# Second block's input projection by Strassen's scheme in 16 of its 18 pairs of column blocks, and its two output projections streamed from DRAM over eight PSUM banks

## The chip, the cores and the metric

One core of a Trainium2 chip runs the whole program. The metric is the device time of one execution in microseconds. The program computes two transformer-like blocks on 1024 positions of width 1024, in float32, with each float32 product made of three matrix products of split operands. Only the middle of the second block is touched here.

## The reference, cut to what matters

```python
def second_block(x, ...):
    h = rms_norm(x, g_mix_pre)
    z = h @ w_in                              # 1024 x 1024 by 1024 x 4608
    u_pool, u_rx, u_rg = z[..., :512], z[..., 512:1536], z[..., 1536:2560]
    gate_pool = sigmoid(z[..., 2560:3584]); gate_rnn = sigmoid(z[..., 3584:])
    y_pool = pool_mixer(u_pool, ...) @ w_pool_out        # 512 wide, by 512 x 1024
    y_rnn = rg_lru_branch(u_rx, u_rg, ...) @ w_rg_out    # 1024 wide, by 1024 x 1024
    x = x + rms_norm((gate_pool * y_pool + gate_rnn * y_rnn) @ w_o, g_mix_post)
    ...                                       # FFN and a last gated term follow

def rg_lru_branch(xb, gb, ...):
    xc = causal_dwconv(xb, conv_w, conv_b)               # 4 taps along the positions
    r, i = sigmoid(xc @ w_gates[0] + b0), sigmoid(xc @ w_gates[1] + b1)   # per head of 64
    log_a = -8 * r * softplus(-lru_lambda); a = exp(log_a)
    u = sqrt(1 - exp(2 * log_a)) * i * xc
    h[t] = a[t] * h[t-1] + u[t]                          # along the positions
    return h * gelu(gb)
```

## The kernel before

Every float32 operand of TensorE is split into a high part, written by ScalarE (`split`, L86), and a low part, made by VectorE as the difference (L89). One product of a 128x128 piece of weights with 512 positions is three matmuls (`mm3`, L341 to L343). Weights come from DRAM into raw buffers (`wr`) through SP's queue, are split into `wh` and `wl`, and a buffer is loaded again as soon as its reader lets it go (`need`, `free`, `pump`). Activations lie transposed, positions along the free axis, as `h2h` and `h2l`. The code is written in Python; a scheduler puts the instructions into one static order for each engine, and each engine then runs its own in that order, waiting on semaphores.

The second block's mixer works on column blocks of `w_in`, 128 columns each, with 8 pieces of 128 rows. A block costs 2 halves of 512 positions x 8 pieces x 3 = 48 matmuls. There are 36 blocks.

- `mixer` (L2041): 16 blocks in pairs, the input `rx` and the gate `gb` of one of 8 groups of recurrent channels, then 4 blocks of the pooling input. `rx` is evicted by ScalarE at L2059, `gb` through a gelu at L2065. After each pair `rnn_chain` (L1917) runs for its 128 channels: a short convolution `xc` (ScalarE L1927, three VectorE operations L1930), its split into `xch` and `xcl`, 12 small matmuls for the two gates, sigmoids (L1943), exp, tanh and square root on ScalarE, a scan on VectorE (L1959), and the product with `gb` on GpSimd (L1960), stored to `zz_d` in DRAM. `pool_chain` (L1964) does the pooling blocks and has 2 float32 matmuls of its own (L1986) for each.
- `mix_gates` (L2071): 16 blocks of gates, through a sigmoid (L2076) to `sg2_d` in DRAM. Meanwhile the 12 pieces of `zz_d` come back and are split into `zh` and `zl`, which hold all of z in SBUF.
- `mix_out` (L2081): for each of 8 output blocks and each half of the positions, 4 pieces of `w_pool_out` and 8 of `w_rg_out`, 576 matmuls in all. Each of the two sums is multiplied with its gate on VectorE (L2109), the two are added (L2111) and split into `m2h`, `m2l`.
- `mix_add` (L2142) multiplies by `w_o`, adds and norms; then `ffn_up` (L2171) starts.

The second half of `ffn_up` already computes pairs of column blocks by a scheme of Strassen's kind. Two column blocks by two halves of the rows of the weights, and two halves of the positions, make a 2x2 problem that takes 7 products of 12 matmuls instead of 8: 84 for 96. In exchange GpSimd makes sums of weights (`wsum`, L238, called S with two operations and D with three), which are split on ScalarE (L227) and VectorE (L228), and the products are combined by two evictions on ScalarE (L2235, L2239), four additions that read PSUM on VectorE and two additions on GpSimd (L2230). The four parts of the weights of a pair are called u, s, d and v. The sums of the activations (`ft1` to `ft3`, and the fourth in place) are made once by `fast_operands` (L262, operations L271 and L272).

Of the kernel before, what the change touches and what calls it, by code (L numbers as in the profile page):

```python
# [16 lines left out]
F32 = mybir.dt.float32  # L18
# [10 lines left out]
P = 128  # L29
# [38 lines left out]
class Kernel:  # L68
# [193 lines left out]
    def fast_operands(self, pool, tmp):  # L262
# [41 lines left out]
        self.fast_last = last  # L304

# [1611 lines left out]
    def rnn_chain(self, pool, c, rx, gb):  # L1917

        nc = self.nc
        t = lambda name, bufs=1, n=S: pool.tile([P, n], F32, name=name, tag=name, bufs=bufs)  # L1920
        wbd = pool.tile([P, 2, P], F32, name="wbd", tag="wbd", bufs=2)
# [4 lines left out]
        xc = t("xc", 2)  # L1926
        nc.scalar.activation(xc, rx[:, 3:], AF.Identity, scale=self.conv_w[:, 24 + c:25 + c],  # L1927
# [4 lines left out]
        xh, xl = (pool.tile([P, S], F32R, name=n, tag=n, bufs=1) for n in ("xch", "xcl"))  # L1932
        self.split(xh, xl, xc)
        wh, wl = (pool.tile([P, 2, P], F32R, name=n, tag=n, bufs=2) for n in ("wgh", "wgl"))
        self.split(wh, wl, wbd)
        yield 6.0
        g = [t("rg0", n=S + 16), t("rg1", n=S + 16)]
# [26 lines left out]
    def pool_chain(self, pool, g, u):  # L1964
# [4 lines left out]
        pw = pool.tile([P, P], F32, name="pw", tag="pw", bufs=2)  # L1969
# [12 lines left out]
        y = pool.tile([P, S], F32, name="py", tag="gb", bufs=2)  # L1982
# [58 lines left out]
    def mixer(self, pl, chunks):  # L2041

        nc = self.nc
        self.sg2_d = self.dram.tile([16, P, S], F32, name="sg2_d")
        self.zz_d = self.dram.tile([12, P, S], F32, name="zz_d")
# [3 lines left out]
        us = {}  # L2049

        def emit(b, half, ps):
            hs = slice(half * 512, half * 512 + 512)
            c = b // 2
            if b < 16 and b % 2 == 0 or b >= 16:
                pad = 3 if b < 16 else 16
                if half == 0:
                    us[b] = pl.tile([P, pad + S], F32, name="rx", tag="rx", bufs=2)
                    nc.gpsimd.memset(us[b][:, :pad], 0.0)
                nc.scalar.activation(us[b][:, pad + half * 512:pad + half * 512 + 512], ps, AF.Copy)  # L2059
                if half and b >= 16:  # L2060
                    self.later_steps(1.0, self.pool_chain(pl, b - 16, us.pop(b)))
            else:
                if half == 0:
                    us[b] = pl.tile([P, S], F32, name="gb", tag="gb", bufs=2)
                nc.scalar.activation(us[b][:, hs], ps, AF.Gelu_apprx_tanh)  # L2065
                if half:
                    self.later_steps(1.0, self.rnn_chain(pl, c, us.pop(b - 1), us.pop(b)))

        return self.dense_t_steps(chunks, self.hT, emit, first=4)

    def mix_gates(self, pl, chunks):  # L2071
        nc = self.nc

        def emit(b, half, ps):
            sg = pl.tile([P, 512], F32, name="sg2", tag="sg2", bufs=2)
            nc.scalar.activation(sg, ps, AF.Sigmoid)  # L2076
            self.later(1.0, lambda: nc.sync.dma_start(self.sg2_d[b, :, half * 512:half * 512 + 512], sg))

        return self.dense_t_steps(chunks, self.hT, emit)

    def mix_out(self, pool, z, chunks, mT):  # L2081

        nc = self.nc
        sgs = []

        def load(n):
            b, half, i = n // 4, n // 2 % 2, n % 2
            sg = pool.tile([P, 512], F32, name="mg", tag="mg", bufs=6)
            nc.sync.dma_start(sg, self.sg2_d[8 * i + b, :, half * 512:half * 512 + 512])
            sgs.append(sg)  # L2090

        for n in range(4):
            load(n)
        for b in range(KT):
            for half in range(2):
                hs = slice(half * 512, half * 512 + 512)
                m = []
                for i, k0 in enumerate((0, 4)):
                    c = chunks[2 * b + i]
                    n = c.shape[1]  # L2100
                    wh, wl = self.need(c)
                    ps = self.mmt()
                    for k in range(n):
                        self.mm3(ps, (wh[:, k], wl[:, k]), (z[0][:, k0 + k, hs], z[1][:, k0 + k, hs]),
                                 k == 0, k == n - 1)
                    if half:
                        self.free(c)
                    sg = sgs.pop(0)
                    nc.vector.tensor_tensor(sg, ps, sg, op=OP.mult)  # L2109
                    m.append(sg)  # L2110
                nc.vector.tensor_add(m[0], m[0], m[1])  # L2111
                self.split(mT[0][:, b, hs], mT[1][:, b, hs], m[0])
                n = 4 * b + 2 * half + 4
                if n < 32:
                    load(n)
                    load(n + 1)
# [54 lines left out]
    def ffn_up(self, pu, up, pairs, es_t, near_end):  # L2171
# [46 lines left out]
        x = self.fast  # L2218

        def product(chunk, o, m):  # L2220
            ps = self.mmt()
            wh, wl = self.need(chunk)
            for k in range(4):
                self.mm3(ps, (wh[:, o + k], wl[:, o + k]), (m[0][:, k], m[1][:, k]), k == 0, k == 3)
            return ps

        for c, (u, s, d, v) in enumerate(pairs, len(up) // 2):
            if c == NC - 2:
                near_end()
            add = lambda e, out, p, q: e.tensor_tensor(out, p, q, op=OP.add)  # L2230
            s1, s2, s3, s5 = (pu.tile([P, 512], F32, name=n, tag=n) for n in ("fs1", "fs2", "fs3", "fs5"))
            new(c)
            g = st[c]
            up0, up1 = (us[c % 2][:, 2 + n * 512:514 + n * 512] for n in range(2))
            nc.scalar.activation(s1, product(u, 0, x["b11"]), AF.Copy)  # L2235
            add(nc.vector, up0, s1, product(u, 4, x["b21"]))
            self.free(u)
            gate(c, 0, up0)
            nc.scalar.activation(s5, product(s, 0, x["t1"]), AF.Copy)  # L2239
            add(nc.vector, s2, s1, product(s, 4, x["t2"]))  # L2240
            self.free(s)
            add(nc.vector, s3, s2, product(d, 0, x["t3"]))
            add(nc.gpsimd, s2, s2, s5)
            add(nc.gpsimd, s5, s3, s5)
            add(nc.vector, up1, s2, product(d, 4, x["b22"]))
            self.free(d)
            gate(c, 1, up1)
            add(nc.vector, s3, s3, product(v, 0, x["t4"]))
            self.free(v)
            nc.vector.tensor_tensor(g[:, half(0)], s3, g[:, half(0)], op=OP.mult)  # L2250
            nc.gpsimd.tensor_tensor(g[:, half(1)], s5, g[:, half(1)], op=OP.mult)
            store(c)
# [18 lines left out]
    def block2(self, es):  # L2271
# [3 lines left out]
        ch_a, es_w, es_c = self.mix_ch, self.es_w, self.es_c  # L2275
        ch_g = [self.chunk_t(blk(wi, 2560 + P * b), KT) for b in range(16)]

        es_h, es_p = (ExitStack() for _ in range(2))
# [3 lines left out]
        with es_c:  # L2282
# [5 lines left out]
            self.queue(ch_a[1:2])  # L2288
# [4 lines left out]
        pl = self.pool(es_p, "mixp")  # L2293
        self.queue(ch_a[2:] + ch_g)
        steps = self.mixer(pl, ch_a)
        for _ in steps:
            pass
        gates = self.mix_gates(sp, ch_g)
        while self.chains or not self.drained("mixw"):
            next(gates)  # L2300
        ch_m = []
        for b in range(KT):
            for w, n in ((a["w_pool_out_2"][0], 4), (a["w_rg_out_2"][0], 8)):
                ch_m += self.chunks_t([blk(w, b * P)], n)
        w = a["w_o_2"][0]
        ch_o = [self.chunks_n(w[:, c * 512:c * 512 + 512], KT, 512) for _ in range(2) for c in range(2)]
        es_p.close()
        es_w.close()

        es_z, es_m = ExitStack(), ExitStack()  # L2310
        zp = self.pool(es_z, "zp")
        z = [zp.tile([P, 12, S], F32R, name=n) for n in ("zh", "zl")]
        k = 0
        with ExitStack() as es2:
            zr = self.pool(es2, "zraw")
# [260 lines left out]
```

## Time and profile before

| what | value |
|---|---|
| median of 3 runs | 3472.66 us (3471.07 to 3474.35) |
| the profiled execution | 3470.65 us, its span 3468.9 us |
| mean granted clock of TensorE | 0.961 |
| mixer's column blocks (recurrent, pooling, gates) | about 1925 to 2348 us of the span |
| `mix_out` | about 2348 to 2487 us |
| `w_o`, its norm and the start of the FFN | about 2487 to 2660 us |
| second half of `ffn_up`, in pairs of 7 products | about 2670 to 3050 us |

Times inside the program are counted from the start of the span. PE is TensorE, DVE VectorE, ACT ScalarE, POOL GpSimd, SP the queue that issues most DMAs. A time that a row gives for one instruction includes its fill; the time between the starts of two that follow each other is shorter.

### The profile page before, as it was taken

The numbers are of one execution on the slowest core, as the hardware profiler recorded it, in microseconds if no ns is written. First come the engines' busy times: TensorE is split into PE (matmuls) and PEld (weight loads), VectorE is DVE, ScalarE is ACT, GpSimd is POOL, SyncE is SP. The second block draws the span as 40 slices with busy tenths as digits, with TensorE's granted clock in tenths as the row PEclk, the third lists the DMA queues.
The fourth block names the chain that finished last, engine by engine and source line by source line (L and its number), as shares of the span: only waits on it lengthen the run. The fifth ranks groups of instructions, "written<-read, shape, count | busy, mean of one in ns | idle before, by whom it ended". The sixth has DMA issues, their size and how long they took to land. (4 is left out here: it accounts for less than half of the span.)

```text
span 3468.9 us, 40965 instructions
## 1 busy us (share of the span) xinstructions
PE 3161.7 (91%) x14129; PEld 2522.5 (73%) x14129; DVE 2298.2 (66%) x3557; ACT 1595.0 (46%) x2396; POOL 1198.3 (35%) x850
## 2 busy tenths in 40 slices
PE   6997799788899789888888999999988999999998
PEld 4875577567678577777666887788767877778787
DVE  7799954668655799999977655313359566563545
ACT  3553212568632566666656674311234333332432
POOL 2133213445303566666642121000021665630114
PEclk9997899899999799999999999999999999999999
DMA  6211377663444899999885221424343222244532
GB/s 195 58 53 58 100 223 207 150 172 88 130 152 168 290 315 318 318 319 322 304 275 181 73 65 66 158 91 128 109 141 96 78 77 77 85 173 155 169 107 75
DMA packets 365087, 548.42 MB, mean 158 GB/s; under 512 B 33292, under 2 KB 184224, under 8 KB 364876
## 3 DMA queue, kind: packets, MB, share of 16 engines
q1 hardware_dynamic: 343744, 503.53, 44.4%
q0 software_dynamic: 11440, 24.77, 2.7%
q10 hardware_dynamic: 9692, 17.48, 1.5%
q8 instruction: 112, 1.84, 0.2%
q14 instruction: 99, 0.81, 0.1%
HBM read 451.63 MB, written 88.78 MB: 156 GB/s over the span
## 5 line engine op out<-in xcount | busy, mean ns | idle before, releaser
L89 DVE TENSOR_TENSOR wl<-wr,wh 128x1024 fp32r<-128x1024 f32 (+1 forms) x489 | 815.4, 1691 | 469.5 <-ACT wh L86 468.7
L86 ACT ACTIVATE wh<-wr 128x1024 fp32r<-128x1024 f32 (+1 forms) x612 | 624.9, 1038 | 577.1 <-PE mm L342 195.4
L89 POOL TENSOR_TENSOR wl<-wr,wh 128x1024 fp32r<-128x1024 f32 x145 | 385.8, 2703 | 91.5 <-ACT wh L86 85.6
L341 PE MATMUL mm<-h2h,wh 128*128 128x512 f32 x576 | 229.4, 399 | 1.2 <-ACT h2h L86 1.2
L343 PE MATMUL mm<-h2h,wl 128*128 128x512 f32 x576 | 227.3, 395 | 0.0
L342 PE MATMUL mm<-h2l,wh 128*128 128x512 f32 x576 | 227.1, 394 | 0.0
L341 PE MATMUL mm<-wh,hTh 128*128 128x512 f32 (+1 forms) x368 | 144.9, 394 | 33.8 <-POOL wh L88 16.0
L343 PE MATMUL mm<-h3h,wl 128*128 128x512 f32 x432 | 170.9, 397 | 5.3 <-DVE wl L89 3.0
L341 PE MATMUL mm<-h3h,wh 128*128 128x512 f32 x432 | 173.8, 404 | 1.6 <-ACT wh L86 1.2
L342 PE MATMUL mm<-h3l,wh 128*128 128x512 f32 x432 | 170.9, 396 | 0.0
L2128 POOL TENSOR_TENSOR max<-max,antmp 128x512 f32<-128x512 f32 x16 | 25.3, 1602 | 391.4 <-DVE antmp L2127 378.2
L342 PE MATMUL pb<-wl,xgh 128*128 128x512 f32 x256 | 109.3, 427 | 48.6 <-DVE wl L89 47.3
L342 PE MATMUL mm<-wl,hTh 128*128 128x512 f32 (+1 forms) x368 | 142.1, 386 | 5.5 <-POOL wl L89 4.9
L343 PE MATMUL mm<-wh,hTl 128*128 128x512 f32 (+1 forms) x368 | 141.5, 384 | 0.0
L1384 POOL TENSOR_SCALAR sm<-sm,src 128x128 f32<-128x128 f32 (+7 forms) x128 | 96.0, 756 | 102.0 <-DVE src L1383 75.9
L341 PEld LDWEIGHTS mm<-h2h,wh 128*128 128x128 f32 x576 | 108.5, 188 | 27.6 <-ACT h2h L86 1.4
L342 PEld LDWEIGHTS mm<-h2l,wh 128*128 128x128 f32 x576 | 108.6, 188 | 26.2 <-issue 1.2
L228 DVE TENSOR_TENSOR wl<-wsum,wh 128x1024 fp32r<-128x1024 f32 x42 | 51.2, 1219 | 114.6 <-ACT wh L227 114.6
L238 POOL TENSOR_TENSOR wsum<-wr 128x512 f32<-128x512 f32 x63 | 90.8, 1455 | 104.0 <-DVE wl L228 54.5
L343 PEld LDWEIGHTS mm<-h2h,wl 128*128 128x128 f32 x576 | 108.4, 188 | 25.2
L341 PE MATMUL mm<-hTh,wh 128*128 128x512 f32 x256 | 106.7, 417 | 19.5 <-POOL wh L88 9.4
L1409 DVE TENSOR_TENSOR ptl<-tr,pth 128x512 fp32r<-128x512 f32 x192 | 102.7, 551 | 27.8 <-ACT pth L1408 26.3
(662 smaller groups left out, 8824.0 us busy)
## 6 DMA issues: line engine op xcount, KB each, us to landing
wr<-in_exp_w SPq DMA_DIRECT2D x384, 512.0 KB
wr<-in_w_in SPq DMA_DIRECT2D x72, 512.0 KB
wr<-in_w_up SPq DMA_DIRECT2D x48, 512.0 KB
wr<-in_w_down SPq DMA_DIRECT2D x48, 512.0 KB
sg_d<-sg SPq DMA_DIRECT2D x64, 256.0 KB
score<-in_ada_w ACTq DMA_DIRECT2D x32, 512.0 KB
hid_d<-fg SPq DMA_DIRECT2D x24, 512.0 KB
wr<-hid_d SPq DMA_DIRECT2D x24, 512.0 KB
```

The source lines that it names most:

```text
L86: self.nc.scalar.activation(hi, x, AF.Copy)
L89: (lo_eng or self.nc.vector).tensor_tensor(lo, x, hi.bitcast(F32), op=OP.subtract)
L228: nc.vector.tensor_tensor(lo, f, hi.bitcast(F32), op=OP.subtract)
L238: gp = lambda i, x, y, op: nc.gpsimd.tensor_tensor(f[:, i], x, y, op=op)
L341: mm(ps, w[0], x[0], start=first, stop=False)
L342: mm(ps, w[0], x[1], start=False, stop=False)
L343: mm(ps, w[1], x[0], start=False, stop=last)
L1384: nc.gpsimd.tensor_scalar(sm, sm, rc[:, l:l + 1], 1.0, op0=OP.mult, op1=OP.mult)
L1409: self.lag.append(lambda c0=c0, th=th, tl=tl, tr=tr: nc.vector.tensor_tensor(tl[:, c0:], tr[:, c0:], th[:, c0:].bitcast(F32), op=OP.subtract))
L2128: nc.gpsimd.tensor_tensor(x[:, cs], x[:, cs], tmp, op=OP.add)
```

## The change

Of the 36 column blocks of `w_in`, four gate blocks stay plain (192 matmuls); behind them `fast_operands` builds the sums of the activations. The other 32 blocks become 16 pairs, each by the 7 products of the new `fast_pair`, which is the body that `ffn_up` had, now shared. A pair is the `rx` and `gb` of a recurrent group ("r"), two gate blocks ("g") or two pooling blocks ("p"), in the order r0 g2 r1 g3 r2 g4 r3 p0 r4 p1 r5 g5 r6 g6 r7 g7. Most tiles of the chains now have one buffer instead of two, and `xch`, `xcl` share the place of `rq`, `rd`. There are 4 pairs of split weight buffers and 2 raw ones in this stage, and one buffer for weight sums.

`mix_out` no longer holds z in SBUF. For each half of the positions it runs through the 4 + 8 row pieces of the two weights; each piece of weights and each two pieces of z are loaded, split and used for 8 output blocks at once, in 8 PSUM banks. The number of matmuls stays 576. The weights are loaded and split twice, once for each half. The sum of the two branches is made on GpSimd.

```diff
+    def fast_pair(self, pool, parts, dest, after):
+        u, s, d, v = parts
...
+        s1, s2, s3, s5 = (pool.tile([P, 512], F32, name=n, tag=n, bufs=1) for n in ("fs1", "fs2", "fs3", "fs5"))
...
+        nc.scalar.activation(s1, product(u, 0, x["b11"]), AF.Copy)
+        ps = product(u, 4, x["b21"])
+        out = dest(0)
+        add(nc.vector, out, s1, ps)
+        self.free(u)
+        after(0, 0, out)
+        nc.scalar.activation(s5, product(s, 0, x["t1"]), AF.Copy)
+        add(nc.vector, s2, s1, product(s, 4, x["t2"]))
+        self.free(s)
+        add(nc.vector, s3, s2, product(d, 0, x["t3"]))
+        add(nc.gpsimd, s2, s2, s5)
+        add(nc.gpsimd, s5, s3, s5)
+        ps = product(d, 4, x["b22"])
+        out = dest(1)
+        add(nc.vector, out, s2, ps)
+        self.free(d)
+        after(0, 1, out)
+        add(nc.vector, s3, s3, product(v, 0, x["t4"]))
+        self.free(v)
+        after(1, 0, s3)
+        after(1, 1, s5)
...
-        xc = t("xc", 2)
+        xc = t("xc", S + 16)[:, :S]
...
-        xh, xl = (pool.tile([P, S], F32R, name=n, tag=n, bufs=1) for n in ("xch", "xcl"))
+        xh, xl = (pool.tile([P, S], F32R, name=n, tag=x, bufs=1) for n, x in (("xch", "rq"), ("xcl", "rd")))
...
+        order = "r0 g2 r1 g3 r2 g4 r3 p0 r4 p1 r5 g5 r6 g6 r7 g7".split()
...
+        def rnn(c, i, n, x):
+            if i:
+                if n == 0:
+                    st["gb"] = tile("gb", "gb")
+                nc.scalar.activation(st["gb"][:, half(n)], x, AF.Gelu_apprx_tanh)
+                if n:
+                    self.later_steps(1.0, self.rnn_chain(pl, c, st["rx"], st["gb"]))
...
+        for j, (z, w) in enumerate(self.out_ch):
+            hs = slice(j // 2 * 512, j // 2 * 512 + 512)
+            ps = [self.trt() for _ in range(3)] + [self.mmt() for _ in range(5)]
+            n = len(w)
+            for k in range(n):
+                (xh, xl), (wh, wl) = self.need(z[k // 2]), self.need(w[k])
+                for b in range(8):
+                    cs = slice(b * P, b * P + P)
+                    self.mm3(ps[b], (wh[:, 0, cs], wl[:, 0, cs]), (xh[:, k % 2], xl[:, k % 2]), k == 0, k == n - 1)
...
+                            nc.vector.tensor_tensor(sg, ps[b], sg, op=OP.mult)
+                            self.later_steps(1.0, rest(b, hs, ms.pop(0), sg))
...
-        with ExitStack() as es2:
-            zr = self.pool(es2, "zraw")
...
-                    self.split(z[0][:, k], z[1][:, k], raw)
...
-            self.add_w(es2, "mow", 1, side="right", only=ch_m)
-            self.mix_out(self.pool(es2, "mixo", side="right"), z, ch_m, mT)
+            self.add_w(es2, "mow", 2, 2, only=self.out_q)
+            self.mix_out(self.pool(es2, "mixo", side="right"), mT)
```

How the engines' orders move, at three places. On TensorE, the matmuls of a recurrent group's gates (`xch`, `xcl`) stand inside a later block. Before, around the first of them for one group:

```order
L343 MATMUL mm<-h2h,wl 128x512
L341 MATMUL mm<-xch,wgh 128x512 x4
L341 MATMUL mm<-h2h,wh 128x512
L342 MATMUL mm<-h2l,wh 128x512
L342 MATMUL mm<-xcl,wgh 128x512
L343 MATMUL mm<-xch,wgl 128x512
L342 MATMUL mm<-xcl,wgh 128x512
L343 MATMUL mm<-xch,wgl 128x512
```

After, in the gate pair that follows the recurrent pair (`ft1` is the third of its seven products):

```order
L382 MATMUL mm<-ft1h,wl 128x512
L380 MATMUL mm<-xch,wgh 128x512 x4
L380 MATMUL mm<-ft1h,wh 128x512
L381 MATMUL mm<-ft1l,wh 128x512
L381 MATMUL mm<-xcl,wgh 128x512
L382 MATMUL mm<-xch,wgl 128x512
L381 MATMUL mm<-xcl,wgh 128x512
L382 MATMUL mm<-xch,wgl 128x512
```

The pattern of the 12 matmuls is the same, but they now stand behind 33 matmuls of the next pair: two products of 12 and 9 of the third.

On ScalarE, at the end of a recurrent pair and the start of the next. Before, from the exp of the last group's gates to the split of the next group's convolution:

```order
L1948 ACTIVATE rq<-rg_17420,sp_9282 128x1024
L86 ACTIVATE wh<-wr 128x1024
L1949 ACTIVATE rg_17420<-rg_17420,sp_9281 128x1024
L2065 ACT_TABLE_LOAD
L2065 ACTIVATE gb<-mm 128x512
L1953 ACT_TABLE_LOAD
L1953 ACTIVATE rg_17420<-rg_17420 128x1024
L86 ACTIVATE xch<-xc 128x1024
```

After, from the table load ahead of the first half of `gb` to the split of the convolution (`fs` are the partial sums of the pair, `wh<-wsum` is the split of a sum of weights, `wh<-wr 128x512` that of v):

```order
L2139 ACT_TABLE_LOAD
L2139 ACTIVATE gb<-fs_17501 128x512
L87 ACTIVATE wh<-wr 128x512
L1966 ACTIVATE xc<-rx,colsb 128x1024
L228 ACTIVATE wh<-wsum 128x1024
L2139 ACTIVATE gb<-fs_17500 128x512
L323 ACTIVATE fs_17633<-mm 128x512
L87 ACTIVATE wh<-wr 128x1024
L87 ACTIVATE xch<-xc 128x1024
```

The convolution `xc` now stands behind a gelu that reads a sum made by GpSimd and behind the split of v; between `xc` and `xch` stand two more splits of weights, the second gelu and an eviction.

On GpSimd, from one group's product with `gb` to the next. Before:

```order
L1960 TENSOR_TENSOR gb<-xc,gb 128x1024
L1950 TENSOR_TENSOR rg_17534<-rg_17534,xc 128x1024
L1922 MEMSET wbd 128x256
L2058 MEMSET rx 128x3
L1960 TENSOR_TENSOR gb<-xc,gb 128x1024
```

After, from the end of a gate pair through most of a recurrent pair (`wsum` in two operations is a sum S, in three a sum D, both for the pair to come; `fs` are the two additions of the running pair):

```order
L1989 TENSOR_TENSOR rg_18034<-rg_18034,xc 128x1024
L322 TENSOR_TENSOR fs_17966<-fs_17966,fs_17968 128x512
L322 TENSOR_TENSOR fs_17968<-fs_17967,fs_17968 128x512
L239 TENSOR_TENSOR wsum<-wr 128x512 x2
L239 TENSOR_TENSOR wsum<-wsum 128x512
L1961 MEMSET wbd 128x256
L1999 TENSOR_TENSOR gb<-xc,gb 128x1024
L239 TENSOR_TENSOR wsum<-wr 128x512
L239 TENSOR_TENSOR wsum<-wsum,wr 128x512
L239 TENSOR_TENSOR wsum<-wr 128x512 x2
L239 TENSOR_TENSOR wsum<-wsum 128x512
L322 TENSOR_TENSOR fs_18160<-fs_18160,fs_18162 128x512
```

The two additions of a recurrent pair now stand behind the sums S and D of the next pair, and those behind `gb` of the group before.

## Rows read from the trace of the kernel before

**Rows 1.** Page, busy microseconds, share of the span and instructions of each engine

```profile
PE 3161.7 (91%) x14129; PEld 2522.5 (73%) x14129; DVE 2298.2 (66%) x3557; ACT 1595.0 (46%) x2396; POOL 1198.3 (35%) x850
```

**Rows 2.** Windows: length, then PE, PEld, DVE, ACT, POOL busy, PEclk, DMA share, GB/s

```profile
2050.00:2100.00 50.00, 50.00 (x219) 40.76 (x218) 27.71 (x26) 35.14 (x41) 11.87 (x7) 1.00 0.21 63
2100.00:2150.00 50.00, 46.19 (x187) 36.05 (x186) 29.05 (x27) 25.50 (x29) 11.81 (x12) 0.93 0.15 49
2750.00:2800.00 50.00, 49.98 (x212) 39.20 (x211) 28.87 (x33) 18.33 (x26) 30.99 (x22) 1.00 0.26 85
```

**Rows 3.** Waits of PE from 1925 to 2490: line, releaser, us in total, times, longest

```profile
PE mm L1986 <- issue: 3.8, 1, 3.8
```

**Rows 4.** Timeline of ACT, evictions: start, duration, what, idle before it

```profile
1993.29 0.60 ACT L2059 ACTIVATE rx<-mm 128x512 f32<-128x512 f32 x1 [3.30 <-PE mm L343]
...
2117.78 0.60 ACT L2059 ACTIVATE rx<-mm 128x512 f32<-128x512 f32 x1 [4.14 <-PE mm L343]
...
2223.13 0.59 ACT L2076 ACTIVATE sg<-mm 128x512 f32<-128x512 f32 x1
...
2245.52 0.60 ACT L2076 ACTIVATE sg<-mm 128x512 f32<-128x512 f32 x1 [4.34 <-issue]
...
2708.02 0.58 ACT L2235 ACTIVATE fs<-mm 128x512 f32<-128x512 f32 x1
...
3045.43 0.58 ACT L2235 ACTIVATE fs<-mm 128x512 f32<-128x512 f32 x1
```

**Rows 5.** Timeline of PE around its one long wait in the mixer

```profile
2140.65 3.75 PE L1986 MATMUL mm<-pd,pw 128*128 128x512 f32 x4 [3.81 <-issue]
...
2145.05 0.63 PE L343 MATMUL mm<-h2h,wl 128*128 128x512 f32 x1
2145.48 0.54 PE L341 MATMUL mm<-h2h,wh 128*128 128x512 f32 x1
```

**Rows 6.** Windows around three of PE's waits, columns as in rows 2

```profile
2140.00:2144.00 4.00, 3.35 (x5) 1.51 (x5) 2.89 (x4) 0.69 (x1) 0.67 (x4) 0.50 0.32 131
...
2500.00:2505.00 5.00, 3.75 (x16) 2.85 (x16) 1.23 (x1) 1.97 (x4) 0.00 (x0) 1.00 0.28 92
...
2630.00:2635.00 5.00, 4.75 (x14) 3.68 (x14) 4.68 (x6) 0.78 (x2) 0.00 (x0) 0.66 0.01 3
```

**Rows 7.** Timeline of a sum S split and the sum D behind it

```profile
2689.97 1.06 ACT L227 ACTIVATE wh<-wsum 128x1024 fp32r<-128x1024 f32 x1 [4.65 <-POOL wsum L238]
...
2691.07 1.23 DVE L228 TENSOR_TENSOR wl<-wsum,wh 128x1024 fp32r<-128x1024 f32 x1 [4.17 <-ACT wh L227]
...
2692.37 2.57 POOL L238 TENSOR_TENSOR wsum<-wr 128x512 f32<-128x512 f32 x2 [2.43 <-DVE wl L228]
...
2695.02 1.29 POOL L238 TENSOR_TENSOR wsum<-wsum 128x512 f32<-128x512 f32 x1
```

**Rows 8.** Groups by line, 2700 to 3040, DVE then POOL: busy, mean ns | idle before

```profile
L2230 DVE TENSOR_TENSOR fs<-fs,mm 128x512 f32<-128x512 f32 x51 | 34.5, 677 | 0.0
L89 DVE TENSOR_TENSOR wl<-wr,wh 128x1024 fp32r<-128x1024 f32 x17 | 30.9, 1816 | 0.0
L238 POOL TENSOR_TENSOR wsum<-wr 128x512 f32<-128x512 f32 x52 | 75.1, 1458 | 43.7 <-DVE wl L228 43.7
L2230 POOL TENSOR_TENSOR fs<-fs,fs 128x512 f32<-128x512 f32 x35 | 45.3, 1293 | 26.8 <-DVE fs L2230 25.5
```

**Rows 9.** Groups by line, 2000 to 2100, POOL, DVE, ACT, columns as in rows 8

```profile
L1960 POOL TENSOR_TENSOR gb<-xc,gb 128x1024 f32<-128x1024 f32 x4 | 13.2, 3293 | 18.4 <-DVE xc L1959 18.4
L1930 DVE SCALAR_TENSOR_TENSOR xc<-rx,colsb,xc 128x1024 f32<-128x1024 f32 x12 | 15.4, 1281 | 0.1
L1927 ACT ACTIVATE xc<-rx,colsb 128x1024 f32<-128x1024 f32 x4 | 4.9, 1236 | 0.0
L86 ACT ACTIVATE xch<-xc 128x1024 fp32r<-128x1024 f32 x4 | 4.3, 1063 | 3.8 <-DVE xc L1930 3.8
```

**Rows 10.** Waits of PE from 2490 to 2660, columns as in rows 3

```profile
PE mm L341 <- ACT wh L86: 2.5, 2, 1.3
```

More of the change, by code (lines that the diff above doesn't have):

```diff
@@ L2069, in mixer @@
[L2069 to L2081, printed above, removed]
+        half = lambda n, pad=0: slice(pad + n * 512, pad + n * 512 + 512)
@@ L2083, in mix_out @@
+        kinds = {"g": (gate_dest, gate), "r": (rnn_dest, rnn), "p": (pool_dest, pooled)}
+        for kind, c, parts in self.mix_fast:
+            dest, after = kinds[kind]
+            self.fast_pair(fp, parts, dest, lambda i, n, x: after(c, i, n, x))
+    def mix_out(self, pool, mT):
         nc = self.nc
@@ L2086, in load @@
         def load(n):
[L2087 to L2092, printed above, removed]
-            load(n)
[L2094 to L2116, printed above, removed]
@@ new lines, in load, with rest @@
+            if n < 32:
+                half, i, b = n // 16, n // 8 % 2, n % 8
+                sg = pool.tile([P, 512], F32, name="mg", tag="mg", bufs=8)
+                nc.sync.dma_start(sg, self.sg2_d[8 * i + b, :, half * 512:half * 512 + 512])
+                sgs.append(sg)
+        def rest(b, hs, m, sg):
+            nc.gpsimd.tensor_tensor(m, m, sg, op=OP.add)
+            yield 3.0
+            self.split(mT[0][:, b, hs], mT[1][:, b, hs], m)
+        for n in range(8):
+            load(n)
@@ L2217, in ffn_up, with finish @@
         es_t.close()
[L2218 to L2227, printed above, removed]
+        def finish(c, i, n, x):
+            g = st[c][:, half(n)]
+            if i == 0:
+                gate(c, n, x)
+            elif n == 0:
+                nc.vector.tensor_tensor(g, x, g, op=OP.mult)
+            else:
+                nc.gpsimd.tensor_tensor(g, x, g, op=OP.mult)
+                store(c)
+        for c, parts in enumerate(pairs, len(up) // 2):
             if c == NC - 2:
                 near_end()
-            add = lambda e, out, p, q: e.tensor_tensor(out, p, q, op=OP.add)
-            s1, s2, s3, s5 = (pu.tile([P, 512], F32, name=n, tag=n) for n in ("fs1", "fs2", "fs3", "fs5"))
             new(c)
[L2233 to L2252, printed above, removed]
+            self.fast_pair(pu, parts, lambda n: us[c % 2][:, 2 + n * 512:514 + n * 512],
+                           lambda i, n, x: finish(c, i, n, x))
     def ffn_down(self, acc, hid, down, half, after):
@@ L2287, in block2 @@
                     next(self.norms)
-            self.queue(ch_a[1:2])
+            self.queue(self.mix_ch[1:2])
             for _ in emb:
@@ L2292, in block2 @@
                 pass
[L2293 to L2304, printed above, removed]
+        fp = self.pool(es_h, "fastp", side="right")
+        self.sums = fq = self.pool(es_w, "mixf")
+        self.later_steps(0.0, self.fast_operands(fp, self.pool(es_t, "mixt")))
+        self.queue(self.mix_ch[2:])
+        self.mix_gates(sp)
+        self.until(lambda: not self.chains)
+        self.fast_last()
+        es_t.close()
+        self.mixer(self.pool(es_p, "mixp"), fq, sp)
+        self.queue(self.out_q)
         w = a["w_o_2"][0]
         ch_o = [self.chunks_n(w[:, c * 512:c * 512 + 512], KT, 512) for _ in range(2) for c in range(2)]
+        self.until(lambda: not self.chains)
+        self.settle()
         es_p.close()
[L2308 to L2313, printed above, removed]
[L2314 to L2324 removed]
         es_h.close()
[L2326 removed]
+        es_m = ExitStack()
         mp = self.pool(es_m, "mT2", side="right")
```

131 lines of the change are left out of this document (87 added, 44 removed).

## The prediction

> **What bounds the kernel now.** I read the busy shares of the page first: TensorE is busy 91% of the span, the next engine 66% [rows 1]. The windows of the second block's mixer say it more sharply: TensorE fills all 50 us of a stretch while VectorE and ScalarE fill 28 and 35 and GpSimd 12 [rows 2]. The table of TensorE's waits, from the first column block of w_in to the end of mix_out, has a single entry of 3.8 us, ahead of a pooling chain's matmuls [rows 3]. So this stage takes as long as its matmuls take, and fewer matmuls are time gained for as long as the other engines keep up. Three spacings in the timeline give the price of a pair of column blocks [rows 4]. Recurrent pairs: five in 2117.78 - 1993.29 = 124.49 us, 24.90 us for 96 + 12 = 108 matmuls, 0.2305 us each. Gates: 2245.52 - 2223.13 = 22.39 us for two blocks, 96 matmuls. Pairs of 7 products in ffn_up: 17 in 3045.43 - 2708.02 = 337.41 us, 19.85 us for 84 matmuls, with TensorE full [rows 2].
>
> **What the change removes.** A recurrent pair should go from 24.90 to 19.85 + 12 x 0.2305 = 22.62 us, 2.28 less; a pooling pair saves as many matmuls, so the same 2.28; a gate pair 22.39 - 19.85 = 2.54. Eight, two and six of them: 18.2 + 4.6 + 15.2 = 38.0 us. The 3.8 us in front of the pooling matmuls go too, since other blocks now stand around them, and with them what followed: the clock stood at 0.50, the 1.2 GHz level, and matmuls were still 0.43 us apart at 2145.05 [rows 5, 6]. From 2140.65 to about 2145.5 at half speed is 2.4 us lost. Gross gain 38.0 + 3.8 + 2.4 = 44.2 us.
>
> **What it adds: the loop of a recurrent and a gate pair.** ffn_up shows such pairs at no cost, but there a pair's results only feed elementwise work. Here they feed a chain whose 12 small matmuls stand 33 matmuls into the next pair. With T = 0 at the start of a recurrent pair and 12 matmuls = 2.8 us, its products end at 2.8, 5.6, ... 19.6, and TensorE wants xch at 19.6 + 33 x 0.233 = 27.3. The sum S of the next pair can be split only when the fourth product has let its buffer go, at 11.2: ScalarE 1.06, VectorE 1.23, and GpSimd starts D at 13.5, as in the rows of ffn_up where D starts 2.4 us after S's split and takes 3.9 [rows 7]. The pair's two additions stand behind D on GpSimd, 1.29 each [rows 8]: they end at 18.7 and 20.0. Then ScalarE: first gelu 0.6 (an eviction of that size takes 0.60 [rows 4]), split of v 0.6, xc 1.24 [rows 9], to 22.45. VectorE: three operations of the convolution with the low part of D's split between them, 3 x 1.25 + 1.2 (starts follow a little closer than the 1.28 of [rows 9]), to 27.6. ScalarE xch 1.06 [rows 9]: 28.7, so TensorE waits 1.4. The four first matmuls and two others cover 1.4 more; xcl stands on VectorE behind an addition 0.7 and a split 1.2, done at 30.75: another 0.7. Together **2.1 us** if nothing disturbs anything.
>
> Something does. The next S runs on GpSimd beside the convolution on VectorE, and where the two meet in ffn_up a split of u takes 1.82 us instead of 1.23 [rows 7, 8]. I add one such 0.6 to 0.7: **2.8 us** per recurrent pair. From below the bound is zero, since nothing in the pairs of ffn_up waits; from above it is 2.1 + 2 x 1.29 = 4.7, both operations of S waited out in full. I take the value next to the measured 0.6. After r4 and r5 the pooling chains' sums and evictions are queued ahead of the chain, one 1.2 and one 0.6 more: 4.5 each. Sum 6 x 2.8 + 2 x 4.5 = 25.8.
>
> **The clock.** A wait costs more if the clock falls after it. After 3.8 us it fell to 0.50; around a wait of 1.3 us it stayed at 1.00; in one stretch by the norms it was 0.66 over 5 us, 1.7 us lost [rows 5, 6, 10]. The new waits come in pieces of about 2 and 1 us. I let two of the eight cost 1.7: 3.4 us, with ends 0 and 13.6.
>
> **The smaller edits.** Start-up: the sums of the activations are about twenty VectorE operations of 1.2 us behind the last transposes, 24 us, while the plain gate blocks give TensorE 192 x 0.2305 = 44 us: cover enough, 0.5 taken for the queue (0 to 3). Mixer to mix_out: the last group's output must be computed, stored and loaded again; its gates' matmuls end at T + 33, some 12 us of sigmoids, exponentials, square root and scan follow, and the GpSimd product of 3.3 us [rows 9] ends near T + 48; the reload stands behind its store on SP's queue, while 22 us of w_pool_out's matmuls need only the pooling pieces, but share that queue: 2 (0 to 5). mix_out itself keeps its 576 matmuls. Twelve more splits of weights cost ScalarE 12 x 1.06 and VectorE 12 x 1.23, hidden beside 24 matmuls = 5.5 us per piece; 768 KB in 5.5 us is 140 GB/s, and 131 ran at a third of the DMA engines [rows 6]. Without that cover each piece would cost its 2.3. At its end eight splits of m2h stand ahead of w_o's third piece on ScalarE and wait for GpSimd's additions, 8 x 1.3 = 10 us against 8 us of matmuls in hand: 3 to 4, where TensorE waited 2.5 for such splits before [rows 10]: 1.5 more (0 to 3). Together 4.0. The other single buffers (gb, rx, wbd) I cost at nothing: each is free some 5 us before its next writer by the schedule above; if a gb store landed late, the gelu and all behind it would move by as much.
>
> **Sum.** -44.2 + 25.8 + 3.4 + 4.0 = -11.0. The profiled execution took 3470.65 us, 2.0 below the median, so 3459.6 by its measure and **3462 us** by the median's. About 0.2%, 7 us, is what a measurement of this kernel can tell from no change.
>
> **Rivals.**
> First, everything is hidden as in ffn_up. For it: VectorE, ScalarE and GpSimd are filled only to 29, 18 and 31 of 50 us there [rows 2], and the scheduler had both chains in view. Against it: the split of S is tied to the fourth product, and D, the additions and the convolution follow one on another, so no free engine shortens it. It gives -44.2 + 4.0: 3470.65 - 40.2 + 2.0 = 3432.
>
> Second, slower: GpSimd and VectorE exclude each other in the loop. The place is the convolution of xc beside S of the coming pair. Each of the 2 operations of S is waited out in full, so 4.7 us per recurrent pair, and such waits bring the clock down each time: 8 x 4.7 + 2 x 1.7 + 8 x 1.7 + 4.0 = 58.6 us, net +14.4, 3487 us. It decides from a wait of 4.6 us per pair with the clock kept, or from 2.9 with the clock lost at each. For it: the 1.82 of the split, the 1.46 mean of a weight sum against 1.29 alone, the 3.29 of gb [rows 7 to 9]. Against it: these rows show half an operation lost, not a whole one. The Trainium skill, in "SBUF — State Buffer", section "SBUF: two separate sides", states the stronger rule: VectorE with two SBUF inputs and a GpSimd operation share a port pair as an exclusive lock, so that the loser "fully blocks". By that rule this rival is the rule of the stage, not its accident; a mean of 1.82 fits a lock that is met half way through.
>
> Third, the waits are as forecast but the clock falls after each, by what it cost in the pooling phase, 2.2 rather than 0.4 on average: 8 x 2.2 = 17.6 instead of 3.4, net +3.2, 3476 us: no change.
>
> **Chances.** Forecast 0.53, its own range 3446 to 3474 (waits of 1.2 to 4 us): 0.42 faster, 0.11 within. First rival 0.17, all faster. Second 0.20, of it 0.15 slower and 0.05 within, since it need not hold in full. Third 0.10, 0.08 within, 0.02 faster. Faster 0.61, within 0.24, slower 0.15. The range leaves out the last few us of the first and second rival: 3436 to 3482.
>
> **What would show it.** In the trace after: about 19.9 us between the first evictions of a gate pair and of the next pair, and 22.6 + 2.8 = 25.4 across a recurrent one with its gates' matmuls; TensorE waits on xch (ScalarE) and on xcl (VectorE) eight times, about 2.8 us in sum each, and no others of size in the pairs. D starting 2.4 us after S's split, and the additions right behind D, show the chain; VectorE's convolution at 1.28 us in the mean speaks against the second rival, at 1.9 for it. Granted clock under 0.9 in windows of the pairs speaks for the third. mix_out should keep TensorE full, at 0.2305 us per matmul. I am wrong if the waits sit elsewhere: on weights (S or D late for the next pair), on transfers, or in mix_out.

## The result: slower, and the profile after

The changed kernel takes 3521.14 us (median of 4 runs, 3518.16 to 3528.82) beside 3472.33 for the kernel before, 48.8 us or 1.4% more; the ratio is 1.0143 (95% interval 1.0126 to 1.0161). The prediction was 3462, faster by some 11 us, with a range of 3436 to 3482. Its profiled execution has a span of 3519.0 us.

TensorE has 192 matmuls fewer and is busy 17 us less [rows 1], yet waits far more. The page's busy times:

```profile
PE 3144.7 (89%) x13937; PEld 2504.3 (71%) x13937; DVE 2470.1 (70%) x3689; ACT 1653.4 (47%) x2462; POOL 1402.0 (40%) x978
```

TensorE's waits from 1900 to 2600, where before the mixer had one of 3.8 us [rows 3] (line, releaser, total, times, longest):

```profile
PE mm L380 <- ACT xch L87: 39.2, 7, 7.2
PE tr L380 <- ACT wh L87: 10.0, 1, 10.0
PE mm L2025 <- DVE pd L2019: 8.4, 1, 8.4
PE mm L2025 <- issue: 7.5, 1, 7.5
PE mm L380 <- ACT wh L87: 4.0, 1, 4.0
...
PE mm L380 <- DVE fs L322: 2.2, 2, 1.6
PE mm L2025 <- ACT gb L2139: 2.2, 1, 2.2
```

The first is the gates' matmuls of seven recurrent groups waiting for `xch`; L2025 are the pooling matmuls; the 10.0 stands 12 us into mix_out, ahead of its third piece of weights, the 4.0 at the start of w_o. Windows (columns as in rows 2): a stretch of the pairs, and 8 us around one wait:

```profile
2050.00:2100.00 50.00, 42.93 (x178) 34.41 (x177) 33.15 (x29) 26.14 (x33) 28.44 (x18) 0.93 0.24 75
...
2036.00:2040.00 4.00, 0.94 (x2) 0.83 (x3) 4.00 (x3) 2.04 (x2) 3.00 (x3) 0.56 0.00 0
2040.00:2044.00 4.00, 4.00 (x12) 3.11 (x11) 1.26 (x2) 2.02 (x4) 0.00 (x0) 0.59 0.18 66
```

No engine is full, and the granted clock falls around this wait, as it does at the other long ones. Where the 50.1 us of span lie, by the first instruction of each stage in both timelines:

| stage | before | after | difference |
|---|---|---|---|
| up to w_in's first matmul | 1912.0 | 1906.2 | -5.8 |
| w_in, chains, gates | 439.7 | 470.8 | +31.1 |
| mix_out | 134.1 | 146.6 | +12.5 |
| w_o to the FFN's first matmul | 104.9 | 112.6 | +7.7 |
| FFN and last term | 878.2 | 882.8 | +4.6 |

In the second row the forecast's gross gain of 44.2 us met 75.3 us of costs. The waits there are 39.2 on xch, 18.1 ahead of the pooling matmuls and 3.4 on sums, xcl and an eviction, 60.7. The other 14.6 fit matmuls at the low clock: added up in the trace, matmuls spaced wider than 0.23 us come to 15.9 us in this stage, 1.5 to 2.7 of it behind each of the six waits of 5 to 7 us on xch and under 1 behind each wait of the pooling matmuls.

### The profile page after: what moved, and what is told of

It is laid out like the page before. It is cut to its first block, busy times and chain, and to the rows that moved or that the text cites. A ratio compares the mean times of both kernels' runs of the same rounds, so it can differ in the third digit from the quotient of the medians.

```text
span 3519.0 us, 41037 instructions
## 1 busy us (share of the span) xinstructions
PE 3144.7 (89%) x13937; PEld 2504.3 (71%) x13937; DVE 2470.1 (70%) x3689; ACT 1653.4 (47%) x2462; POOL 1402.0 (40%) x978
## 3 DMA queue, kind: packets, MB, share of 16 engines
q1 hardware_dynamic: 336192, 509.82, 44.2%
q8 instruction: 111, 1.82, 0.2%
## 5 line engine op out<-in xcount | busy, mean ns | idle before, releaser
L87 ACT ACTIVATE wh<-wr 128x1024 fp32r<-128x1024 f32 x632 | 641.1, 1032 | 556.1 <-PE mm L381 152.3
L239 POOL TENSOR_TENSOR wsum<-wr 128x512 f32<-128x512 f32 x111 | 173.2, 1573 | 200.4 <-DVE wl L229 104.7
L228 ACT ACTIVATE wh<-wsum 128x1024 fp32r<-128x1024 f32 x74 | 77.9, 1053 | 197.9 <-POOL wsum L239 186.9
L380 PE MATMUL mm<-wh 128*128 128x512 f32 x360 | 142.8, 397 | 0.0
L381 PE MATMUL mm<-wl,wh 128*128 128x512 f32 x360 | 142.5, 396 | 0.0
L382 PE MATMUL mm<-wh,wl 128*128 128x512 f32 x360 | 141.9, 394 | 0.0
L322 POOL TENSOR_TENSOR fs<-fs,fs 128x512 f32<-128x512 f32 x74 | 103.3, 1395 | 64.4 <-DVE fs L322 61.5
L380 PE MATMUL mm<-h2h,wh 128*128 128x512 f32 x320 | 126.7, 396 | 1.6 <-ACT h2h L87 1.2
L382 PE MATMUL mm<-h2h,wl 128*128 128x512 f32 x320 | 126.2, 394 | 0.0
L381 PE MATMUL mm<-h2l,wh 128*128 128x512 f32 x320 | 125.9, 394 | 0.0
```

Of the source, the lines that this page charges most:

```text
L87: self.nc.scalar.activation(hi, x, AF.Copy)
L228: nc.scalar.activation(hi, f, AF.Copy)
L239: gp = lambda i, x, y, op: nc.gpsimd.tensor_tensor(f[:, i], x, y, op=op)
L380: mm(ps, w[0], x[0], start=first, stop=False)
L381: mm(ps, w[0], x[1], start=False, stop=False)
L382: mm(ps, w[1], x[0], start=False, stop=last)
```

## One period, followed back

`xch` is split at 1987.18, 2037.95, 2088.82 and 2139.84: a recurrent and a gate pair repeat every 50.9 us, where 180 matmuls at 0.2305 us need 41.5. TensorE starts this recurrent pair at 2004.6 = T. On GpSimd (timeline: start, duration, what, idle before):

```profile
2013.71 3.31 POOL L1999 TENSOR_TENSOR gb<-xc,gb 128x1024 f32<-128x1024 f32 x1 [3.71 <-DVE xc L1998]
2016.99 2.30 POOL L239 TENSOR_TENSOR wsum<-wr 128x512 f32<-128x512 f32 x1
2019.36 1.29 POOL L239 TENSOR_TENSOR wsum<-wsum,wr 128x512 f32<-128x512 f32 x1
2023.09 2.55 POOL L239 TENSOR_TENSOR wsum<-wr 128x512 f32<-128x512 f32 x2 [2.43 <-DVE wl L229]
2025.72 1.29 POOL L239 TENSOR_TENSOR wsum<-wsum 128x512 f32<-128x512 f32 x1
2026.97 2.68 POOL L322 TENSOR_TENSOR fs<-fs,fs 128x512 f32<-128x512 f32 x2
```

On ScalarE and VectorE:

```profile
2020.69 1.06 ACT L228 ACTIVATE wh<-wsum 128x1024 fp32r<-128x1024 f32 x1 [6.16 <-POOL wsum L239]
...
2029.68 0.63 ACT L2139 ACTIVATE gb<-fs 128x512 f32<-128x512 f32 x1 [6.63 <-POOL fs L322]
...
2030.74 1.23 ACT L1966 ACTIVATE xc<-rx,colsb 128x1024 f32<-128x1024 f32 x1
...
2037.95 1.06 ACT L87 ACTIVATE xch<-xc 128x1024 fp32r<-128x1024 f32 x1 [3.09 <-DVE xc L1969]
...
2088.82 1.06 ACT L87 ACTIVATE xch<-xc 128x1024 fp32r<-128x1024 f32 x1 [3.09 <-DVE xc L1969]
```

```profile
2011.35 2.28 DVE L1998 TENSOR_TENSOR_SCAN xc<-rd,rq 128x1024 f32<-128x1024 f32 x1
...
2034.40 3.51 DVE L1969 SCALAR_TENSOR_TENSOR xc<-rx,colsb,xc 128x1024 f32<-128x1024 f32 x2
...
2051.81 2.32 DVE L229 TENSOR_TENSOR wl<-wsum,wh 128x1024 fp32r<-128x1024 f32 x1
...
2054.65 1.72 DVE L1995 SCALAR_TENSOR_TENSOR rq<-rq,rg 128x1024 f32<-128x1024 f32 x1
2056.29 1.78 DVE L90 TENSOR_TENSOR wl<-wr,wh 128x512 fp32r<-128x512 f32 x1
...
2058.05 1.46 DVE L90 TENSOR_TENSOR wgl<-wbd,wgh 128x256 fp32r<-128x256 f32 x1
2059.43 2.31 DVE L1997 TENSOR_TENSOR rq<-rq,rg 128x1024 f32<-128x1024 f32 x1
```

And TensorE at the wait itself:

```profile
2031.49 0.40 PE L382 MATMUL mm<-ft1h,wl 128*128 128x512 f32 x1
2039.06 2.07 PE L380 MATMUL mm<-xch,wgh 128*128 128x512 f32 x4 [7.17 <-ACT xch L87]
```

The scan of the group before ends at 2013.6, gb at 2017.0 = T + 12.4, and only then can GpSimd begin S, which ScalarE splits at T + 16.1 where the forecast had T + 11.2. From there the forecast's chain runs as written, 4.9 us late and 0.8 slower in the convolution: xch at T + 34.4 for the 28.7 foreseen. The gates' matmuls, their sigmoids and the next scan follow, and with them the next gb and S. So the pairs form a closed loop: 26.6 us from the start of a scan (2011.35) to the start of the split of xch (2037.95), 24.3 from there to the start of the next scan (2062.26).

## Experiments

Theories: **loop** (the period is the sum of that chain's links; shorten a link and the period follows, down to TensorE's bound), **contention** (GpSimd and VectorE slow each other, whatever the order), **placement** (the gates' matmuls merely stand too early). Differences are between medians, each against the kernel before run beside it on the same chip; e4 and e8 are single runs. The period is the median of the three spacings between the splits of xch of the first four groups, in the profiled execution. The text compares two changed kernels by their differences from the kernel before.

| run | time | against before | period, us |
|---|---|---|---|
| changed kernel | 3521.1 | +48.8 | 50.9 |
| e1 | 3482.3 | +14.3 | 45.0 |
| e2 | 3488.9 | +20.9 | 46.9 |
| e3 | 3478.8 | +10.9 | 45.1 |
| e4 | 3512.1 | +44.2 | 49.3 |
| e5 | 3463.3 | -6.6 | 42.1 |
| e6 | 3477.0 | +7.1 | 45.0 |
| e7 | 3466.4 | -3.6 | 47.1 |
| e8 | 3523.4 | +53.4 | 50.8 |
| e9 | 3498.8 | +28.4 | 47.5 |
| e10 | 3453.9 | -16.4 | 41.7 |
| e11 | 3513.8 | +43.5 | 50.3 |
| e12 | 3458.1 | -12.2 | 42.0 |

**e4 and e1: cutting the link from gb to S.**

```diff
-        nc.gpsimd.tensor_tensor(gb, xc, gb, op=OP.mult)
+        nc.vector.tensor_tensor(gb, xc, gb, op=OP.mult)
```

and in e1 also `tag="wsum", bufs=2` for `bufs=1`.

> Only the first of the two edits: gb on VectorE, one sum buffer. Loop theory: S leaves GpSimd's queue behind gb, but still waits until VectorE has split the sum D before it, which stands behind the scan; gain 1 to 2 us per period, 3503 to 3513 us in all. If GpSimd's gb alone was the link, the period falls by its full 3.3 us: below 3497.

> Two edits on the changed kernel: the product of the scan with gb moves from GpSimd to VectorE, and the weight sums of the mixer get two buffers (two instead of three for the stored gates make the room). Loop theory: recurrent and gate pair repeat every 50.9 us because the sum S of a gate pair stands on GpSimd behind gb of the group before and waits for the one sum buffer; with both gone S is ready before the fourth product ends, its split moves from 2020.7 to about 2015.8, the wait on xch falls from 7.2 to about 2.3 us, the period to 46, and the time to 3470 to 3485 us. Contention theory (GpSimd and VectorE slow each other whatever the order): the same amount of work overlaps, the period stays at 49 to 51 and the time at 3510 to 3521. Placement theory (the gates' matmuls just stand too early): xch comes when it came, no change.

e4 gained 1.5 us per period, as the loop theory had it: S left the queue behind gb but still waited for the one sum buffer. Its 5 us in all (9 beside the changed kernel's median) are a single run's and not clear of noise. With that buffer doubled too, e1 came to 45.0 us per period, 34.5 us below the changed kernel. e4 and e1 do the same work on every engine and differ in buffers alone, yet the period falls by 4.3 us; so it is the order that counts, not the amount of work that overlaps. The waits of e1 in the first four groups are 0.7 to 1.5 us on xch and 1.7 on xcl, 2.4 to 3.2 together. The forecast had 2.1 undisturbed and 2.8 with a collision, so its size for this pair was about right once S comes early, with more of it on xcl than the 0.7 foreseen. The waits of e1, 1900 to 2560:

```profile
PE mm L381 <- DVE xcl L90: 10.0, 7, 1.7
PE mm L2025 <- DVE pd L2019: 8.1, 1, 8.1
...
PE mm L380 <- ACT xch L87: 6.9, 5, 2.3
```

**e2: only the place.** `yield 6.0` becomes `yield 12.0` ahead of the gates' matmuls.

> The changed kernel with one number altered: the 12 matmuls of a recurrent group's gates are issued 6 us later in the program's own clock, so some 28 matmuls further into the next pair. Placement theory: the waits of 7.2 us on xch shrink by about 6 us each, the time falls by 40 to 50 us to about 3475. Loop theory: what follows the gates' matmuls is moved as well, S of the next gate pair is later by the same amount, and the wait reappears ahead of the product with the sum S; the period stays within 1.5 us of 50.9 and the time within 12 us of 3521.

Neither number came. The waits on xch shrank from 39.2 to 4.6 us in all, but 9.7 on xcl came in their place; no product waited for S; the period fell by 4.0 us and the time by 27.9. From scan to xch it is 26.6 us as before (2059.07 to 2085.67), from xch to the scan 20.3 instead of 24.3: with the matmuls later, the splits of S and v that had stood between two steps of the chain on VectorE now stand ahead of it. So the place of the matmuls counts too, more than the loop theory allowed. A loop whose links include what is queued between the steps fits this; that reading was made after the run.

```profile
PE mm L2025 <- DVE pd L2019: 17.7, 2, 10.4
PE mm L381 <- DVE xcl L90: 9.7, 6, 1.8
...
PE mm L380 <- ACT xch L87: 4.6, 5, 2.0
```

**e3: gate pairs without sums.** Gate pairs call a plain product of two column blocks. In this kernel those read activations in which one quarter holds the fourth sum, so its gates aren't the reference's; the work is the same.

> The changed kernel with the six pairs of gate blocks as plain products, 96 matmuls each for 84, and so without their sums of weights and of products; recurrent and pooling pairs stay as they are. Loop theory: the loop is cut, since a gate pair needs no S or D; a recurrent and a gate pair take 22.6 + 22.4 = 45.0 us and little wait, 5.9 less than 50.9 in six places, 3480 to 3490 us although there are 72 more matmuls. Contention theory: the GpSimd work falls by a third, waits shrink by a third, 3515 or more with the matmuls added.

45.1 us per period and 37.9 us less, with 72 matmuls more, as the loop theory said.

**e11: more work for TensorE.** One more `product(v, 0, x["t4"])` in recurrent pairs.

> The changed kernel with one product of 12 matmuls done twice in each recurrent pair, ahead of its seventh, its first result unused: 96 matmuls more, 22 us of TensorE at full clock. Loop theory: they stand where TensorE later waits, so they fill the wait; it falls from 7.2 to about 4.4 us, the period stays within 0.7 us of 50.9 and the time within 5 us of 3521. If TensorE's own work set the pace, the period grows by 2.8 us and the time by 18 to 22.

The period stayed, 50.3, and 96 more matmuls cost nothing; the time came out 5 us lower, with intervals that overlap (1.0113 to 1.0144 here). TensorE's own work does not set the pace. The wait on xch fell from 39.2 to:

```profile
PE mm L382 <- ACT xch L87: 17.6, 6, 4.1
```

**e5: the loop cut and the matmuls moved**, e1 with `yield 10.0`.

> The two edits of e1 together with a milder form of e2 (the gates' matmuls issued 4 us later in the program's clock, about 18 matmuls). In e1 the period was 45.0 us with waits of 1.2 to 1.5 us on xch and 1.7 us on xcl left. Loop theory: with the loop cut those 2.9 us are a matter of place alone, so here they go, the period comes to 42.5 to 43.5 us, what 180 matmuls need, and the time to 15 to 22 us below e1: about 3460 to 3467 us beside 3468 for the kernel before. Contention theory: the split of xc comes late by what GpSimd takes from VectorE, whatever the place, and moving the matmuls brings less than 8 us.

As expected, the period even a little shorter: 42.1 us, and 6.6 us below the kernel before (ratio 0.9982, interval 0.9967 to 0.9997). What is left stands outside the loop (waits, 1900 to 2680):

```profile
PE mm L2025 <- DVE pd L2019: 18.2, 2, 12.0
...
PE mm L381 <- DVE xcl L90: 5.2, 5, 2.8
...
PE mm L380 <- ACT xch L87: 0.6, 1, 0.6
```

**e9: the additions of a pair off GpSimd.**

```diff
-        add(nc.gpsimd, s2, s2, s5)
-        add(nc.gpsimd, s5, s3, s5)
+        eng = nc.vector if self.nsum == 2 else nc.gpsimd
+        add(eng, s2, s2, s5)
+        add(eng, s5, s3, s5)
```

`nsum` is 2 in the mixer and 1 in `ffn_up`; here it only picks the engine, and the sum buffer stays single.

> The changed kernel with one edit: the two additions that end a pair's sums run on VectorE, right behind the addition they follow, instead of on GpSimd, where they stand behind the sums S and D of the next pair. Loop theory: that takes them out of the chain from S to xc. They end near 2024.3 instead of 2029.7, then the split of D (GpSimd until 2027.0) is the later of the two inputs of the convolution, xch comes 5 to 6 us earlier, the period falls from 50.9 to 45 to 46 us and the time by 32 to 45 us, 3475 to 3488. Contention theory: VectorE has 1.4 us more work per pair and GpSimd 2.7 less; the period moves by under 1.5 us, 3510 to 3525.

The direction is the loop's, the size half to two thirds: 3.4 us of period instead of 5 to 6, 20.4 us of time instead of 32 to 45. gb still stands ahead of S; and the two additions, 0.69 us each alone, took 3.00 together beside D. Contention has its part.

**e7: one part alone.** All pairs plain and no sums, mix_out streamed.

> One part of the change alone: all 36 column blocks as plain products (1728 matmuls as before), in the new order of groups and gates and with the new single buffers, and the new mix_out that streams z and the weights. By the changed kernel's trace mix_out and the start of w_o cost 20 us more than before, of it 10 + 4 us of waits ahead of them that need not appear here in full; the mixer without sums should run at 47.3 us per recurrent and gate pair with no wait. So 8 to 20 us above the kernel before, 3476 to 3488. If the streamed mix_out is free, within 4 us of it.

A miss, and a telling one: 3.6 us below the kernel before (0.9985, interval 0.9973 to 0.9997). mix_out takes 132.5 us there for 134.1 before, so streaming z costs nothing in this run, where the last chain ends 3.1 us into mix_out, and the single buffers do no harm at 47.1 us per period. The stage of w_in is 7.8 us shorter than before, with no wait left ahead of the pooling matmuls in the new order; the stage of w_o is 5.7 us longer (110.6 for 104.9), with 3.9 us of wait at its start. So the loss, but for some 6 us at w_o, needs the fast pairs and the chains beside them. A window of e7:

```profile
2050.00:2100.00 50.00, 50.00 (x218) 40.81 (x217) 21.33 (x17) 26.30 (x30) 7.46 (x5) 1.00 0.24 76
```

**e8 and e6: the start of mix_out.** In e8 the store of a group goes through `nc.gpsimd.dma_start`; e6 is e5 with that, the additions of mix_out on VectorE and the pooling matmuls 4 us later.

> The changed kernel with one edit: the recurrent results are stored from GpSimd's queue, right behind the product that makes them. If the wait of 10 us ahead of mix_out comes from loads of z that stand behind the last store on SP's queue, it falls to under 4 us and the time to 3509 to 3514 us. If the store and reload of the last group itself set it, it stays at 8 or more.

> e5 with three more edits for the waits outside the loop: the recurrent results are stored to DRAM from GpSimd's queue instead of SP's, the additions of mix_out run on VectorE instead of GpSimd, and the pooling chains' matmuls are issued 4 us later. If the 10 us ahead of mix_out come from loads of z queued behind the last store on SP, 4 us ahead of w_o from splits queued behind GpSimd's additions, and 16 us ahead of the pooling matmuls from VectorE's queue, each falls by half or more: 12 to 20 us below e5, 3442 to 3455 us. If the reload itself is what takes the time, the first stays and the gain is under 10 us.

e8 came out at 3523.4 us, and the wait stays, 10.2 us. z now passes, but the next weights do not: SP waits for the last group's store to land before it may load (waits of TensorE, and of SP's queue, e8):

```profile
PE tr L380 <- ACT wh L87: 10.2, 1, 10.2
```

```profile
SPq L197 <- DMA zz_d<-gb: 7.4, 1, 7.4
```

That the new raw buffers lie where the mixer's tiles were fits this, but was not tried apart. e6 missed: 7.1 us above the kernel before where 12 to 20 below e5 were expected; the period went from 42.1 back to 45.0, and the pooling phase only changed the instruction that waits. The longer period points to the store: in the traces of e5 and e6 every engine runs the same instructions in the same order through the first four groups, but for the store, which in e6 stands on GpSimd, 0.55 us long, ahead of a pair's additions. How 0.55 us become 3 was not followed up; in e8, where the same edit was made to the changed kernel, the period stayed at 50.8. e6's largest waits:

```profile
PE mm L381 <- DVE xcl L90: 11.4, 6, 2.9
PE mm L380 <- DVE fs L322: 9.5, 1, 9.5
PE tr L380 <- ACT wh L87: 8.1, 1, 8.1
```

**e10 and e12: put together.** e5 with both kinds of additions on VectorE; e12 has gb back on GpSimd.

> e5, with the additions of a pair on VectorE as in e9 and the additions of mix_out on VectorE. The period is at TensorE's bound in e5 already, so the first brings nothing there; it can shorten the waits of the pooling phase (18 us in e5) by a few us. The second should halve the wait of 4.0 us ahead of w_o. 2 to 8 us below e5: 3455 to 3462 beside 3470 for the kernel before.

> e10 but with the product of the scan and gb left on GpSimd, behind which S then stands again, with two buffers for the sums. Loop theory: with the additions off GpSimd the link from gb to S is short of the bound by itself, S still comes after gb, and xch is ready no later than the moved place of the matmuls wants it: within 6 us of e10. If gb ahead of S was the whole trouble, the waits on xch come back by 2 us and more each, 15 us or more above e10.

e10 has the lowest median of the study, 16.4 us below the kernel before (0.9960, interval 0.9947 to 0.9974) and 65 below the changed one. Its first pairs run at TensorE's bound:

```profile
2050.00:2100.00 50.00, 50.00 (x218) 40.76 (x217) 45.24 (x42) 30.91 (x36) 33.63 (x17) 1.00 0.27 88
```

The wait ahead of w_o is down to 0.6 us, the one in mix_out to 2.8. e12 lies 4.2 us above e10, with the same interval (0.9947 to 0.9974), so no difference is shown: gb ahead of S alone is harmless once the other links are short and the sums have two buffers. Left in e10, with 192 matmuls saved, are 17.4 us ahead of the pooling matmuls:

```profile
PE mm L2026 <- DVE pd L2020: 17.4, 2, 11.3
```

## Why the prediction was wrong

**What bounds the kernel, and the gain.** Right. 44.2 us fits the books of the stage, and in e10 a recurrent and a gate pair take 41.7 us for the 42.5 I worked out.

**The loop.** This step failed. The forecast followed the chain forward from S and took S to wait for its buffer alone, at T + 11.2. It put gb of the group before at about T + 48 of its own pair, by some 12 us of work behind the gates' matmuls. The last of those matmuls ends at 2044.5 us, T + 39.9, and gb ends 23.4 us later, where the forecast had 15: between the steps stand the splits of the next S and v and of a gate matrix, the running pair's additions and D, and many of them collide. The five operations of VectorE shown from 2051.81 to 2059.43 and gb together took 5.7 us more than the same operations undisturbed, so about two thirds of these 8.4 us are collisions; this is an estimate from durations. So gb ends at T + 63, in the next pair, S follows it on GpSimd, and the wait is 7.2 where I had 2.1 to 2.8. I checked one turn of the loop and not whether it closes within the 42 us of a period. Terms: waits of the loop 42 us (xch, xcl, sums) and ahead of the pooling matmuls 18.1, where the forecast had 25.8 in all.

**The collision.** Also mis-sized, and by a wrong reading. The 1.82 us of a split against 1.23 [rows 7, 8] I took for half an operation lost. Single rows of the kernel before say otherwise. All 17 splits of that group take 1.81 to 1.83 us, and each begins 0.73 us before a GpSimd addition ends and waits for that end. The first of them, and the two additions of which the second is running:

```profile
2703.70 1.82 DVE L89 TENSOR_TENSOR wl<-wr,wh 128x1024 fp32r<-128x1024 f32 x1
```

```profile
2701.77 2.67 POOL L2230 TENSOR_TENSOR fs<-fs,fs 128x512 f32<-128x512 f32 x2
```

So 0.6 is what was left of the other operation, not a rate, and the loss can be nearly a whole one: after, 2.32 and 2.31 for operations of 1.23 above, 2.30 for a sum of 1.29. The convolution's mean came to 1.51 us, between the 1.28 and the 1.9 named as signs. A clean case stands in e7, where little runs on GpSimd; VectorE, then GpSimd:

```profile
2040.11 1.23 DVE L90 TENSOR_TENSOR wl<-wr,wh 128x1024 fp32r<-128x1024 f32 x1 [3.57 <-ACT wh L87]
...
2051.07 3.04 DVE L90 TENSOR_TENSOR wl<-wr,wh 128x1024 fp32r<-128x1024 f32 x1 [0.57 <-ACT wh L87]
```

```profile
2050.64 2.39 POOL L2018 TENSOR_TENSOR gb<-xc,gb 128x1024 f32<-128x1024 f32 x1 [11.33 <-issue]
```

The split that starts inside gb ends 1.1 us after gb ends, at 2054.1. By the Trainium skill, "SBUF — State Buffer", section "SBUF: two separate sides", the two engines share a port pair as an exclusive lock; these rows agree, and I gave that rival too little.

**Rivals.** The second, slower, was the nearest and had the right direction, at a chance of 0.15. Its place, the convolution beside S, cost 0.8 us of collision where it had 2.6; it priced collisions in one link, 3487 us, and not the loop that passes on those of every link. The amount of collisions does not set the period. Taking each operation's shortest time over the traces as its undisturbed one, VectorE and GpSimd together ran 14.0 us longer per period in the changed kernel, 14.3 in e1, 8.4 in e11 and 17.7 in e10, whose periods are 50.9, 45.0, 50.3 and 41.7. What counts is which collisions stand on the loop.

**The clock.** 3.4 us forecast, about 15 measured: the waits of 5 to 7 us bring the clock down each time, at a price of some 2 us, near the third rival's 2.2. In e1, whose waits in the first groups are of the forecast's own size (0.7 to 1.7 us each), they cost 0.1 us each that way.

**The smaller edits.** 4.0 forecast. mix_out cost 12.5 (10.0 of wait and the low clock behind it), w_o 7.7, its wait of 4.0 within the 3 to 4 foreseen. The forecast saw both queues. In the changed kernel SP issues the first load of z right behind the last group's store, at 2385.99 and 2385.56 us, 9 us into mix_out. In e5 the last chain ends as late (8.9 us into mix_out for 8.6), but that load is issued 7.8 us ahead of the store, and the wait is 3.5; why it comes earlier there was not tried. The -5.8 ahead of the mixer and +4.6 at the end lie within what the traces of the other runs show: w_in's first matmul stands between 1905.8 and 1916.6 us, the last row between 876 and 883.

**The pooling phase.** Forecast as 1.7 us more for each of two groups, with nothing ahead of the pooling matmuls themselves, it took 18.1 there. In e5 the eviction of the second pooling input waits 7.3 us for the recurrent group's gb, whose single buffer of xc it takes; this is read from the trace and was not tried alone.

## What to carry to other kernels

A chain that runs from one stage's result back into the queues that feed the next stage is a loop: follow it until it meets itself, and compare its length, with all that is queued between its steps, to the period that the bound engine needs. A saving on the full engine is lost when it shortens the period below that length, and adding work to that engine is then free as long as it fits into its waits, which is the quick test (e11). An operation that takes longer than its undisturbed kind may be waiting out the rest of another; look at the single instruction and at what ran when it began, before half an effect is priced.

## What the hardware showed

A VectorE operation on two SBUF inputs and a GpSimd operation did not share time: the one that came second waited the other out, 1.23 to 3.04 us beside a GpSimd operation of 2.39. Where a VectorE operation that reads SBUF alone began inside a GpSimd operation, it ran longer by what that one had left, less 0.1 to 0.2 us: in all 59 cases of the changed kernel's mixer, all 7 of e7's and all 35 among the pairs of the kernel before. The additions that read PSUM, five in each pair of column blocks and not four as in the section on the kernel before, kept 0.67 to 0.69 us in all 34 such cases after. The granted clock stood at 0.56 to 0.59, near the lower of its two levels (1.2 of 2.4 GHz), around a wait of 7.2 us, the matmuls behind it 0.43 us apart for about 4 us, although TensorE had been busy without a gap for 43 us before.
